# The second gate's sums in the tiles of the bias b2, and half of the last weight chunk in the tiles of the output sums

## The chip, the core and the metric

The kernel runs on one core of a Trainium2 chip. Its engines work side by side, each through its own queue of instructions in order: TensorE (PE, matrix products into the PSUM memory, with PEld for its weight loads), VectorE (DVE), ScalarE (ACT), GpSimd (POOL) and SyncE (SP, which here only issues transfers). The metric is the time of one execution on the device in microseconds (us). A difference of half a per cent, some 5.7 us here, is about what measurements of this kernel can tell from none.

## What is computed

The reference is one layer of an encoder over 256 tokens of width 2048 in float32: windowed attention, then a squared-ReLU MLP with 8192 hidden columns. Each half is scaled and shifted by vectors worked out from a condition `c`, gated by another such vector, added to `alpha * x` and normalised. What the change touches is the second half:

```python
mod = c_act @ mod_w[i] + mod_b[i]
sh_m, sc_m, g_m, sh_f, sc_f, g_f = jnp.split(mod, 6, axis=-1)
...
hff = x * (1.0 + sc_f[:, None, :]) + sh_f[:, None, :]
y = sq_relu_mlp(hff, mlp_w1[i], mlp_b1[i], mlp_w2[i], mlp_b2[i])
x = layer_norm(DEEPNORM_ALPHA * x + (1.0 + g_f[:, None, :]) * y, ln_mlp_g[i], ln_mlp_b[i])
```

The second gate is `g_f`, a product of the condition with a 2048 x 2048 matrix. The bias b2 is `mlp_b2`. The output sums are `y`.

## The kernel before

**Precision.** Every float32 factor is split into a high part (ACT casts it, line 254) and a low part (DVE subtracts the high part from the original, line 225). A product is then two or three fp32r matmuls: `mm3` (lines 497 to 500) is high x high, high x low, low x high.

**The weight stream.** `Stream` (lines 181 to 285) holds one long list of chunks, each 128 x 2048 floats (1 MB), in the order in which they are used. SP loads them into the pool `raws`, which has five buffers at this stage (`loads`, line 203). A chunk of weights is split in two halves of 128 x 1024, whose high and low parts go to the pools `whp` and `wlp` with five buffers each (NHIGH and NLOW, lines 41 and 42). So weights can be up to five halves ahead of TensorE. `pump` (line 230) walks the list; `stop` is a place in it that `pump` does not pass. A chunk planned with `kept` puts its halves into tiles of the pool `g4` and not into the rings, and is split only when it is asked for.

**Modulation chunks.** Chunks of the modulation matrices stand in the same list with a function `use`, which is `Mod.step` (line 322). For the second gate, `m_gf`, all 16 chunks are summed on DVE: two instructions of 128 x 1024 for each chunk (lines 351 to 353), one into each of the two tiles of `part`. Before the first of them, `step` clears the two tiles on POOL (line 334) and loads the gate's bias into row 0 of each through ACT's queue (line 335). `gate` (line 385) later splits the sums, adds up the 128 rows with matmuls and writes the gate into two tiles.

**The MLP** is cut into four blocks of 2048 hidden columns (BLK = 4). The hidden columns of block 0 are worked out first (lines 999 to 1029). Then come, for each block, `ff_hidden` (line 1031, not for block 0) and four calls of `ff_out` (line 1059), one for each chunk c of 512 output columns. One `ff_out` is 96 matmuls of 512 columns: four weight chunks (kg), each with four rows of k, two token tiles t and the three matmuls of `mm3`. Its two sums lie in two PSUM banks out of the pool `psa`, which has five. They are added into the output sums `ys` (lines 1079 to 1083), together with b2 in block 0 (line 1081). The 16 chunks of the gate stand among the weights of block 1, and `gate` is called in block 2 after its second hidden group (line 1048).

**The last chunk** (lines 1112 to 1129) takes c = 3 of block 3 apart: all four weight chunks are asked for, then the whole sum of t = 0 is written, gated, normalised and sent out, then that of t = 1.

**Two pools of tiles of 128 x 1024.** `g4` has 20 buffers. In the last chunk, 8 of them hold the hidden columns (`us`), 4 the residual `xs` and 4 the rows of the last norm (`gb`, line 1092); 4 are left. `g4b` has six buffers and is opened in the memory of early load buffers (line 66). At the MLP it is asked for the four tiles of `ys` (line 1069), two for b2 (line 1070), two for the gate's sums (line 332) and two for the gate itself (line 387).

**Who sets the order.** The order on each engine is not that of the code. A scheduler goes through a model of the run when the program is built: an instruction is put on its engine's queue when its inputs are there in the model and its output tile has a buffer, the earlier in the code first. A tile gets its buffer when its first writer comes up, and gives it back after its last reader. `ORDER_ONLY` edges and `pinned` hold some orders in earlier stages, not here.

Of the kernel before, what the change touches and what calls it, by code (L numbers as in the profile page):

```python
# [12 lines left out]
F32R = mybir.dt.float32r  # L13
# [7 lines left out]
S = 256  # L21
# [9 lines left out]
BLK = 4  # L31
# [16 lines left out]
def hybrid_kernel(ctx: ExitStack, tc: tile.TileContext, a, out: bass.AP):  # L48
# [4 lines left out]
    whp = ctx.enter_context(tc.tile_pool(name="whp", bufs=NHIGH))  # L53
    wlp = ctx.enter_context(tc.tile_pool(name="wlp", bufs=NLOW))
# [11 lines left out]
    def g4b(dt=F32):  # L66
        if not more:
            early.close()
            more.append(ctx.enter_context(tc.tile_pool(name="gen2", bufs=2 * MORE)))
        return more[0].tile([128, 1024], dt, tag="g4b", name="g4b")  # L70

    def g4(dt=F32):
        return gen.tile([128, 1024], dt, tag="g4", name="g4")
# [96 lines left out]

        return add

    def bias_all(src, g4=g4):

        b = [g4(), g4()]
        for h in range(2):
            nc.gpsimd.dma_start(b[h], src[:, h * 1024:h * 1024 + 1024].partition_broadcast(128))
        return lambda c: b[c // 2][:, (c % 2) * 512:(c % 2) * 512 + 512]


    class Stream:
# [15 lines left out]
            self.prev = None  # L197
            self.side = {}

        def plan(self, src, use=None, kept=False):  # L200
            self.q.append((src, use, kept))

        def loads(self):
# [17 lines left out]
        def low(self):  # L221
            n = len(self.ls)
            r, kept = self.src[n]
            l = g4(F32R) if kept else wlp.tile([128, 1024], F32R, name="wl")
            self.pinned(nc.vector.tensor_sub(l, r, f32(self.hs[n])))  # L225
            self.ls.append(l)
            if n % 2:
                self.freed(self.of[n])

        def pump(self, vecs, must=0):  # L230

            while len(self.ls) < must or self.at < len(self.q):
                self.loads()
                n = len(self.hs)
                if len(self.ls) < n - 1 and len(self.ls) - self.used < self.nl or len(self.ls) < min(must, n):
                    self.low()
                    continue
                if self.at >= len(self.q) or self.at == self.stop:
                    return
                assert self.at < len(self.raw)  # L240
                src, use, kept = self.q[self.at]
                if use is not None:
                    if not vecs and n >= must:
                        return
                    vecs = max(vecs - 1, 0)
                    use(self.raw[self.at])
                    self.at += 1
                    self.freed(self.at - 1)
                    continue
                if n >= must and (n - self.used >= self.nh or kept):  # L250
                    return
                h = g4(F32R) if kept else whp.tile([128, 1024], F32R, name="wh")
                s = self.raw[self.at][:, n % 2 * 1024:n % 2 * 1024 + 1024]
                self.pinned(nc.scalar.copy(h, s))  # L254
                self.hs.append(h)
                self.src.append((s, kept))
                self.of.append(self.at)
                self.at += n % 2
# [28 lines left out]
    S = Stream()  # L287
# [4 lines left out]
    class Mod:  # L292
# [29 lines left out]
        def step(self, raw):  # L322
            w, kc, i = self.w, self.kc, self.i
            if i == 0:
                self.ps = psm.tile([128, 512], F32, name="pm")
            r = raw.rearrange("p (k j n) -> p k j n", k=kc // 2 if self.pairs else kc, j=4)
            self.i += 1
            last = self.i == self.n
            per = 1024 // w
            if i == self.start:  # L330

                self.part = [(g4b if self.whole else g4)() for _ in range(2)]
                for n, p in enumerate(self.part):
                    nc.gpsimd.memset(p, 0.0)
                    nc.scalar.dma_start(p[0:1], self.bias[:, n * 1024:n * 1024 + 1024])
            for k in range(kc):
                kt = i * kc + k
                if self.pairs:
                    if k % 2 == 0:
                        cols = [cact[:, kt + j // 2:kt + j // 2 + 1].to_broadcast([128, 32]) for j in range(4)]  # L340
                        self.quad(cols, [r[:, k // 2, j] for j in range(4)], last and k == kc - 2)
                elif i in self.dve:
                    e = min(4 * w, 1024)
                    new = self.part is None
                    if new:
                        self.part = [g4() for _ in range(4 * w // e)]
                    for n, p in enumerate(self.part):
                        s = raw[:, k * 4 * w + n * e:k * 4 * w + n * e + e]
                        if new:
                            nc.vector.tensor_scalar(p[:, :e], s, cact[:, kt:kt + 1], None, op0=OP.mult)  # L350
                        else:
                            nc.vector.scalar_tensor_tensor(p[:, :e], s, cact[:, kt:kt + 1], p[:, :e],  # L352
                                                           op0=OP.mult, op1=OP.add)
                else:
                    stop = last and k == kc - 1 and not self.dve
                    self.quad(cact[:, kt:kt + 1].to_broadcast([128, 32]), [r[:, k, j] for j in range(4)], stop)
            if last and not self.whole:
                if self.dve:
                    self.quad(onesf[:, :32], [self.part[j // per][:, (j % per) * w:(j % per) * w + w]
                                              for j in range(4)], True)  # L360
                self.r = sml.tile([128, 512], F32, name="mrow", bufs=2)
                nc.scalar.copy(self.r[:, :w], self.ps[:, :w])
# [116 lines left out]
    for blk in range(BLK):  # L479
        for f in range(NF):  # L480
            if blk:
                if blk == 1 and f % 2:
                    m_gf.plan()
                S.plan(a["w1b"][(blk - 1) * NF + f])
        for c in range(4):
            for kg in range(4):
                if blk == 1 and kg % 2:
                    m_gf.plan()
                S.plan(a["w2"][blk, c, kg], None, blk == BLK - 1 and c == 3 and kg > 1)


    acc, xts, held, xs = {}, {}, {}, []
# [390 lines left out]
    for n in range(21):  # L883
        j, i = n // 4, n % 4
        if n < 16:
            scores(n)
        for f in todo:
            f()
        todo = []
        if n == 1:  # L890
            S.deep = False
        if n == 5:
            assert all(h is raws for h in S.home[S.at:]), "an early buffer is still in use"
        if n + 2 < len(LATE):
            w = qkv(*LATE[n + 2])
        elif n < 5:
            w = iter((0, 1))
        else:
            if n == 5:
                ys, bo = [g4b() for _ in range(4)], bias_all(a["bo"], g4b)  # L900
            w = project((n - 5) // 4, (n - 5) % 4)
        S.vecs(SLOT_FILL.get(n, 0) if len(LATE) - 2 <= n < 5 else 0)
        mid = mids(n)
        if j < 3:
            if i == 0:
                turn = rope(j + 1, 1)
            if i < 3:
                mid.append(lambda: qA.__setitem__(j + 1, next(turn)))
            if i == 2:
                mid.append(lambda: qhl.__setitem__(j + 1, split_q(qA[j + 1])))  # L910
            if i == 3:
                for h in range(2):
                    mid.append(lambda h=h: qT.__setitem__((j + 1, h), q_heads(qhl[j + 1], h)))
        run(w, mid)
        if 0 < n <= 16 and n % 2 == 0:
            todo.append(values(n - 1))
        if n == 12:
            g1 = gate(m_gm)
        if n == 16:
            warm = sml.tile([128, 1], F32, name="warm")  # L920
            nc.scalar.activation(warm, eps, AF.Sqrt)
            st = [sml.tile([128, 4, 6], F32, name=f"st{t}", bufs=2) for t in range(NT)]
# [144 lines left out]
        return pss  # L1067

    ys = [g4b() for _ in range(4)]
    bf = bias_all(a["b2"], g4b)  # L1070
    for blk in range(BLK - 1):
        if blk:
            us = ff_hidden(blk)
        for c in range(4):
# [9 lines left out]
            if blk == 1:  # L1084
                for t in range(NT):
                    z = part(xs, t, c)
                    nc.vector.scalar_tensor_tensor(z, z, ALPHA, gb[0], op0=OP.mult, op1=OP.mult)
                    nc.vector.scalar_tensor_tensor(z, gb[1], ALPHA, z, op0=OP.mult, op1=OP.add)

    blk = BLK - 1  # L1090
    us = ff_hidden(blk)
# [120 lines left out]
```

## Time and profile before

| what | us |
|---|---|
| median of three runs | 1139.51 (1135.54 to 1139.8) |
| the profiled execution, whole | 1136.72 |
| its span, first to last instruction | 1135.0 |
| TensorE busy | 1088.9 (96% of the span) |
| VectorE busy | 811.0 (71%) |
| ScalarE busy | 546.7 (48%) |
| GpSimd busy | 21.7 (2%) |
| block 0's `ff_out`, c = 0 evicted | 511.8 |
| the first and the last of the 16 loads of the gate's matrix issued | 550.0, 720.7 |
| the last chunk of block 3 begins | 1096.0 |
| TensorE's last matmul begins | 1118.2 |

The profiled execution's 1136.72 us are 1.72 us more than its span. In rows of the timeline, the columns are the start, the duration, the engine, the line of the kernel, the operation, what it writes and reads (the tile's name in the program), how many instructions the row merges, and in brackets how long the engine was idle before and what ended that. A tile of `g4` is shown as `g`, one of `g4b` as `g4b`, a PSUM bank of `psa` as `pa`. A queue's own instruction has a q behind the engine's name. In rows of stages, each engine has its busy time within the stretch and in parentheses its instructions; then come TensorE's granted clock (1.00 is full), the share of the DMA engines' time and GB/s.

### The profile page before, as it was taken

How to read it: one execution, taken by the hardware profiler on the slowest of the kernel's cores; microseconds unless marked ns; L12 is line 12 of the kernel's file. 1: busy time of each engine (PE TensorE's matmuls, PEld its weight loads, DVE VectorE, ACT ScalarE, POOL GpSimd, SP SyncE). 2: the span in 40 equal slices, each digit the busy share in tenths (PEclk: the TensorE clock that was granted, in tenths of full speed). 3: DMA queues.
4: the chain of work that ended last, by engine and by line, in shares of the span. 5: the costliest groups of instructions: out<-in, count | busy, mean ns of one | idle time of the engine just before them, and what ended most of it. 6: DMA issues, size and time to landing. Idle time of an engine off the chain costs nothing.

```text
span 1135.0 us, 15765 instructions
## 1 busy us (share of the span) xinstructions
PE 1088.9 (96%) x6250; PEld 880.2 (78%) x6250; DVE 811.0 (71%) x1121; ACT 546.7 (48%) x852; POOL 21.7 (2%) x40
## 2 busy tenths in 40 slices
PE   8889999799999999999999999999999999999994
PEld 6657667466677699988888887878888888888883
DVE  5587896778899878765577888746666556665656
ACT  5333445676775455553444543335444344444431
POOL 2000000000000000000000010000000000000001
PEclk9999999999999999999999999999999999999997
DMA  9999995656886798655578788854555555557512
GB/s 374 419 420 418 421 392 196 253 186 255 322 305 258 276 366 313 207 187 186 196 290 296 263 303 319 303 206 155 187 187 186 185 190 193 186 187 268 200 38 75
DMA packets 42570, 288.50 MB, mean 254 GB/s; under 512 B 4720, under 2 KB 5360, under 8 KB 8704
## 3 DMA queue, kind: packets, MB, share of 16 engines
q1 hardware_dynamic: 39824, 279.85, 66.8%
q0 software_dynamic: 1792, 6.29, 1.7%
q10 hardware_dynamic: 880, 1.35, 0.3%
q8 instruction: 49, 0.80, 0.3%
q14 instruction: 25, 0.20, 0.0%
HBM read 285.38 MB, written 2.10 MB: 253 GB/s over the span
## 4 chain that ended last, share of the span: by engine, by line
PE 82%; DMA 7%; DVE 6%; ACT 3%; issue 1%; DVEq 0%; ACTq 0%; SPq 0%
PE pa L1042 15%; PE pa L498 14%; PE pa L500 14%; PE pa L499 14%; PE pa L1043 8%; DMA raw<-in_modm 4%; PE pm L314 3%; PE pa L1019 3%; PE pa L1018 3%; PE pa L1020 3%; DVE wl L225 2%; PE pa L789 1%; DMA raw<-in_wqkv 1%; PE pt L774 1%; ACT wh L254 1%
## 5 line engine op out<-in xcount | busy, mean ns | idle before, releaser
L225 DVE TENSOR_TENSOR wl<-raw,wh 128x1024 fp32r<-128x1024 f32 x332 | 404.5, 1224 | 242.0 <-ACT wh L254 241.4
L254 ACT CAST wh<-raw 128x1024 fp32r<-128x1024 f32 x332 | 348.1, 1055 | 457.9 <-PE pa L500 246.9
L498 PE MATMUL pa<-wh,g 128*128 128x512 f32 x816 | 321.5, 395 | 10.9 <-ACT g L534 3.4
L500 PE MATMUL pa<-wh,g 128*128 128x512 f32 x816 | 318.9, 392 | 1.7 <-DVE g L536 1.7
L499 PE MATMUL pa<-wl,g 128*128 128x512 f32 x816 | 319.5, 392 | 0.0
L1042 PE MATMUL pa<-g,wh 128*128 128x512 f32 x768 | 271.8, 399 | 2.9 <-DVE rl L991 2.9
L1043 PE MATMUL pa<-g,wl 128*128 128x256 f32 x768 | 215.7, 281 | 0.0
L498 PEld LDWEIGHTS pa<-wh,g 128*128 128x128 f32 x816 | 153.5, 188 | 52.0 <-issue 6.0
L500 PEld LDWEIGHTS pa<-wh,g 128*128 128x128 f32 x816 | 153.2, 188 | 38.5 <-DVE g L536 3.6
L499 PEld LDWEIGHTS pa<-wl,g 128*128 128x128 f32 x816 | 153.6, 188 | 32.6 <-issue 2.6
L1042 PEld LDWEIGHTS pa<-g,wh 128*128 128x128 f32 x768 | 144.3, 188 | 39.5 <-DVE rl L991 3.6
L1043 PEld LDWEIGHTS pa<-g,wl 128*128 128x128 f32 x768 | 145.1, 189 | 0.2
L1019 PE MATMUL pa<-g,wh 128*128 128x256 f32 x256 | 72.7, 285 | 0.4 <-DVE g L962 0.4
L1018 PE MATMUL pa<-g,wh 128*128 128x256 f32 x256 | 72.5, 286 | 0.0
L1020 PE MATMUL pa<-g,wl 128*128 128x256 f32 x256 | 72.2, 283 | 0.0
L352 DVE SCALAR_TENSOR_TENSOR g<-raw,cact,g 128x1024 f32<-128x1024 f32 x53 | 68.0, 1283 | 0.4
L314 PE MATMUL pm<-raw,cact 128*32 128x256 f32 (+2 forms) x832 | 54.8, 379 | 5.4 <-DMA raw<-in_modm 4.4
L1018 PEld LDWEIGHTS pa<-g,wh 128*128 128x128 f32 x256 | 48.7, 192 | 1.3 <-issue 0.8
L1019 PEld LDWEIGHTS pa<-g,wh 128*128 128x128 f32 x256 | 49.1, 192 | 0.9 <-DVE g L962 0.8
L1020 PEld LDWEIGHTS pa<-g,wl 128*128 128x128 f32 x256 | 49.1, 192 | 0.0
L352 DVE SCALAR_TENSOR_TENSOR g4b<-raw,cact,g4b 128x1024 f32<-128x1024 f32 x32 | 40.6, 1282 | 7.5 <-DMA raw<-in_modgf 5.2
L314 PEld LDWEIGHTS pm<-raw,cact 128*32 128x32 f32 x832 | 21.6, 109 | 27.8 <-issue 12.3
(174 smaller groups left out, 836.7 us busy)
## 6 DMA issues: line engine op xcount, KB each, us to landing
raw<-in_w SPq DMA_DIRECT2D x64, 1024.0 KB, 4.9
raw<-in_w1b SPq DMA_DIRECT2D x48, 1024.0 KB, 4.9
raw<-in_modm SPq DMA_DIRECT2D x32, 1024.0 KB, 14.7
raw<-in_modf SPq DMA_DIRECT2D x32, 1024.0 KB, 7.1
raw<-in_wqkv SPq DMA_DIRECT2D x24, 1024.0 KB, 15.2
raw<-in_modgm SPq DMA_DIRECT2D x16, 1024.0 KB, 6.0
raw<-in_wo SPq DMA_DIRECT2D x16, 1024.0 KB, 5.8
raw<-in_w1a SPq DMA_DIRECT2D x16, 1024.0 KB, 8.1
```

The lines of the kernel that those rows point to most:

```text
L225: self.pinned(nc.vector.tensor_sub(l, r, f32(self.hs[n])))
L254: self.pinned(nc.scalar.copy(h, s))
L314: i = nc.tensor.matmul(self.ps[32 * j:32 * j + 32, :w], lhsT[j] if type(lhsT) is list else lhsT, rhs[j], start=self.first, stop=stop)
L352: nc.vector.scalar_tensor_tensor(p[:, :e], s, cact[:, kt:kt + 1], p[:, :e], op0=OP.mult, op1=OP.add)
L498: nc.tensor.matmul(ps, xh, wh, start=start, stop=False)
L499: nc.tensor.matmul(ps, xh, wl, start=False, stop=False)
L500: S.prev = nc.tensor.matmul(ps, xl, wh, start=False, stop=stop).ins
L1018: nc.tensor.matmul(o, wh(w, 128), hh, start=new, stop=False)
L1019: nc.tensor.matmul(o, wh(w, 128), hl, start=False, stop=False)
L1020: nc.tensor.matmul(o, wl(w, 128), hh, start=False, stop=end)
L1042: nc.tensor.matmul(ps, wh(k, 128), hb, start=k == 0, stop=False)
L1043: nc.tensor.matmul(ps[:, :256], wl(k, 128), hb[:, :256], start=False, stop=k == NK - 1)
```

## The change

- `bias_all` gets its two tiles from its caller instead of taking them from a pool.
- The two tiles of the gate's sums are taken where the output sums are, ahead of block 0, and b2 is loaded into the same two tiles. `step` no longer takes tiles for the second gate; it clears those two when its first chunk comes up, which is after the last read of b2.
- So that the clearing stands behind the reads of b2 in the code, `pump` stops at the gate's first chunk (`first_gf`) until block 0 is through.
- `kept` becomes a number. Of the last weight chunks (block 3, c = 3), kg = 2 goes to `g4` as before (1) and kg = 3 to `g4b` (2).

```diff
-    def bias_all(src, g4=g4):
-
-        b = [g4(), g4()]
+    def bias_all(src, b):
+
         for h in range(2):
             nc.gpsimd.dma_start(b[h], src[:, h * 1024:h * 1024 + 1024].partition_broadcast(128))
...
-            l = g4(F32R) if kept else wlp.tile([128, 1024], F32R, name="wl")
+            l = (g4, g4b)[kept - 1](F32R) if kept else wlp.tile([128, 1024], F32R, name="wl")
...
-                h = g4(F32R) if kept else whp.tile([128, 1024], F32R, name="wh")
+                h = (g4, g4b)[kept - 1](F32R) if kept else whp.tile([128, 1024], F32R, name="wh")
...
             if i == self.start:
 
-                self.part = [(g4b if self.whole else g4)() for _ in range(2)]
+                if not self.whole:
+                    self.part = [g4() for _ in range(2)]
                 for n, p in enumerate(self.part):
                     nc.gpsimd.memset(p, 0.0)
                     nc.scalar.dma_start(p[0:1], self.bias[:, n * 1024:n * 1024 + 1024])
...
                 if blk == 1 and f % 2:
+                    if f == 1:
+                        first_gf = len(S.q)
                     m_gf.plan()
...
-                S.plan(a["w2"][blk, c, kg], None, blk == BLK - 1 and c == 3 and kg > 1)
+                S.plan(a["w2"][blk, c, kg], None, max(kg - 1, 0) if blk == BLK - 1 and c == 3 else 0)
...
-                ys, bo = [g4b() for _ in range(4)], bias_all(a["bo"], g4b)
+                ys, bo = [g4b() for _ in range(4)], bias_all(a["bo"], [g4b(), g4b()])
...
     ys = [g4b() for _ in range(4)]
-    bf = bias_all(a["b2"], g4b)
+    m_gf.part = [g4b(), g4b()]
+    bf = bias_all(a["b2"], m_gf.part)
+    S.stop = first_gf
     for blk in range(BLK - 1):
...
                     nc.vector.scalar_tensor_tensor(z, gb[1], ALPHA, z, op0=OP.mult, op1=OP.add)
+        S.stop = 0
```

More of the change, by code (lines that the diff above doesn't have):

```diff
@@ L198, in __init__, with plan @@
             self.side = {}
-        def plan(self, src, use=None, kept=False):
+        def plan(self, src, use=None, kept=0):
             self.q.append((src, use, kept))
```

## The prediction

> **What bounds the kernel now.** I read the page's head first, then the stages.
>
> ```profile
> span 1135.0 us, 15765 instructions
> PE 1088.9 (96%) x6250; PEld 880.2 (78%) x6250; DVE 811.0 (71%) x1121; ACT 546.7 (48%) x852; POOL 21.7 (2%) x40
> ```
>
> ```profile
> 500.00:1080.00 580.00, 574.77 (x2872) 485.68 (x2872) 383.62 (x455) 255.52 (x311) 7.40 (x13) 1.00 0.64 223
> 680.00:700.00 20.00, 17.64 (x78) 14.27 (x78) 16.66 (x20) 6.35 (x6) 1.34 (x3) 1.00 0.91 323
> 760.00:780.00 20.00, 17.13 (x94) 14.19 (x93) 13.13 (x20) 11.47 (x18) 0.00 (x0) 1.00 0.39 136
> 1120.00:1136.00 16.00, 0.00 (x0) 0.00 (x0) 11.22 (x19) 1.56 (x3) 3.27 (x2) 0.59 0.35 131
> ```
>
> TensorE sets the time. In the MLP (500 to 1080) it is idle for 580.00 - 574.77 = 5.23 us only. The two 20 us stretches hold all of that: 2.36 and 2.87 us. Behind its last matmul comes a tail in which DVE works. So the change can win those 5.23 us and a part of the tail, and nothing else in the MLP. Next, what ends each gap in the timeline of TensorE, and where block 0's sums are evicted (line 1081) in that of DVE, with the gate's reading of its sums (line 392), and the clearings of these sums on POOL:
>
> ```profile
> 693.45 0.50 PE L498 MATMUL pa<-wh,g 128*128 128x512 f32 x1 [2.36 <-DVE g4b L1083]
> 765.92 0.50 PE L1042 MATMUL pa<-g,wh 128*128 128x512 f32 x1 [2.61 <-DVE rl L991]
> 773.73 0.50 PE L1042 MATMUL pa<-g,wh 128*128 128x512 f32 x1 [0.26 <-DVE rl L991]
> ```
>
> ```profile
> 511.77 1.28 DVE L1081 TENSOR_TENSOR g4b<-pa,g4b 128x512 f32<-128x512 f32 x2
> 533.54 1.28 DVE L1081 TENSOR_TENSOR g4b<-pa,g4b 128x512 f32<-128x512 f32 x2
> 555.29 1.28 DVE L1081 TENSOR_TENSOR g4b<-pa,g4b 128x512 f32<-128x512 f32 x2
> 769.13 1.28 DVE L1081 TENSOR_TENSOR g4b<-pa,g4b 128x512 f32<-128x512 f32 x2
> 770.33 1.28 DVE L1083 TENSOR_TENSOR g4b<-g4b,pa 128x512 f32<-128x512 f32 x2
> L392 DVE TENSOR_TENSOR g<-g4b,g x4: 684/686/692, 767.3 to 773.6; 128x512 fp32r<-128x512 f32 x4
> ```
>
> ```profile
> 383.59 0.95 POOL L334 MEMSET g4b<- 128x1024 f32 x1 [40.29 <-issue]
> 534.88 0.96 POOL L334 MEMSET g4b<- 128x1024 f32 x1 [150.33 <-DVE g4b L1081]
> ```
>
> Three evictions come 21.76 us apart, so the fourth was due at 555.29 + 21.76 = 577.1. It comes at 769, 192 us late. The clearings tell why. `g4b` has six buffers: b2 held two, the gate's first sum took one at 383.59, three chunks of `ys` the rest; the buffer that b2 gave back at 534.8 went to the second sum. So the fourth chunk of `ys` had no buffer until the gate had read its sums (from 767.3). Until then block 0's sums for c = 3 stayed in **two of the five banks** of `psa`, and from 757 on block 1's in two more. TensorE therefore waited for a bank: at 691 between c = 0 and c = 1 (two sums end, two begin, three banks), at 763 between two hidden groups with one bank left, and briefly at 773.
>
> **Part 1: sums and b2 share tiles.** Now `g4b` is asked for 2 + 4 tiles, which is six: the fourth eviction finds its buffer and comes at about 577, and all five banks go round. The first and second wait need a shortage of banks, so both should go: 2.36 + 2.61. The third stands where `gate` asks for four banks more; I count it as gone too, 0.26, since the evictions at 769 and 770 (2.4 us of DVE just ahead of it) leave that place. Ends for these gaps: 0 won (each comes back) and 5.23; I take **-5.2**. DVE does the same work.
>
> What is added is a wait. The second tile is read by block 0 until the fourth eviction ends, 577.1 + 1.28 = 578.4. Only then can it be cleared and its bias row loaded:
>
> ```profile
> 555.78 1.06 ACT L254 CAST wh<-raw 128x1024 fp32r<-128x1024 f32 x1 [1.66 <-PE pa L500]
> 555.79 0.56 ACTq L335 DMA_DIRECT2D g4b<-in_modgfb x2
> 558.50 1.06 ACT L254 CAST wh<-raw 128x1024 fp32r<-128x1024 f32 x1 [1.66 <-PE pa L500]
> ```
>
> ```profile
> 556.87 1.23 DVE L225 TENSOR_TENSOR wl<-raw,wh 128x1024 fp32r<-128x1024 f32 x1 [0.30 <-ACT wh L254]
> 560.26 1.29 DVE L352 SCALAR_TENSOR_TENSOR g4b<-raw,cact,g4b 128x1024 f32<-128x1024 f32 x1 [2.16 <-DMA g4b<-in_modgfb]
> 563.73 1.28 DVE L352 SCALAR_TENSOR_TENSOR g4b<-raw,cact,g4b 128x1024 f32<-128x1024 f32 x1
> 555.41 7.63 SPq L209 DMA_DIRECT2D raw<-in_w1b x2
> 565.04 0.33 SPq L209 DMA_DIRECT2D raw<-in_modgf x1
> ```
>
> The time to landing of all loads into `g4b`, and of the gate's chunks:
>
> ```profile
> DMA to landing us min/median/max: 5.3/6.3/7.4
> DMA to landing us min/median/max: 6.4/6.9/7.5
> ```
>
> 578.4 + 0.96 (POOL) = 579.3 for the issue from ACT's queue; the bias was in use 4.5 us after its issue before, and the loads of `g4b` (this row has the large ones too) took up to 7.4: the second sum can start at 584 to 587. Before, it started at 563.73. Three queues feel this. ACT has the issue between its casts. DVE may stand at the waiting sum, as it did for 2.16 us ahead of 560.26; the 580 us stretch shows no TensorE idle time for that. SP's queue feels it most: the load at 565.04 began when the sum at 563.73 gave its buffer back. With the gate's first chunk in its buffer until 586 + 1.3, the next loads of the gate pile up in the five buffers, and the weights pass through three or two. I followed the list through: each weight buffer is given back every 5.44 us (two halves of 558.50 - 555.78 = 2.72); from f = 1 at 555.4 on, f = 2 goes out at 561, the gate's second chunk at 566, f = 3 at 572, f = 4 at 577, the gate's third at 582.5, and f = 5 only with the release near 588, some 11 us late. TensorE needs f = 5 at 577.1 + 5 x 5.44 = 604.3; its first half needs 1.06 (ACT), 1.23 (DVE) and a load of up to 7.5: issue by 594.5. That leaves **6 us**, so I cost the wait at 0. Cover: five halves of weights ahead, 13.6 us. If it were gone, every us of lateness would be one of TensorE. [...]
>
> The stop itself costs nothing that I can find: the casts above are released by TensorE giving back a buffer, not by their place in the code, and the gate's first tile (b2's columns of c = 0 and 1, read by 534.8) can be cleared 44 us ahead of the second.
>
> **Part 2: kg = 3 in the tiles of `ys`.** The tail, by the timelines of ACT, PE and DVE, and line 1101, the last reader of `ys`:
>
> ```profile
> 1105.71 1.06 ACT L254 CAST g<-raw 128x1024 fp32r<-128x1024 f32 x1 [11.18 <-PE pa L500]
> 1110.10 1.06 ACT L254 CAST g<-raw 128x1024 fp32r<-128x1024 f32 x1 [3.33 <-PE pa L500]
> ```
>
> ```profile
> 1095.99 0.39 PE L498 MATMUL pa<-wh,g 128*128 128x512 f32 x1
> 1101.43 0.39 PE L498 MATMUL pa<-g,g 128*128 128x512 f32 x1
> 1104.15 0.39 PE L498 MATMUL pa<-wh,g 128*128 128x512 f32 x1
> 1113.84 0.62 PE L500 MATMUL pa<-g,g 128*128 128x512 f32 x2
> 1118.15 0.39 PE L500 MATMUL pa<-g,g 128*128 128x512 f32 x1
> ```
>
> ```profile
> 1114.27 0.69 DVE L797 TENSOR_TENSOR tmp<-pa,g4b 128x512 f32<-128x512 f32 x1 [1.52 <-PE pa L500]
> 1119.78 0.69 DVE L797 TENSOR_TENSOR tmp<-pa,g4b 128x512 f32<-128x512 f32 x1
> 1120.38 3.08 DVE L1127 SCALAR_TENSOR_TENSOR g<-g,r,g 128x512 f32<-128x512 f32 x3
> 1123.38 0.68 DVE L798 TENSOR_TENSOR g<-g,tmp 128x512 f32<-128x512 f32 x1
> 1128.28 3.08 DVE L1127 SCALAR_TENSOR_TENSOR g<-g,r,g 128x512 f32<-128x512 f32 x3
> ```
>
> ```profile
> L1101 DVE TENSOR_TENSOR g4b<-g4b x8: 685/686/689, 875.9 to 943.5; 128x512 f32<-128x512 f32 x8
> ```
>
> The last two casts wait for TensorE to free tiles of `g4` (four were left, kg = 2 has them). So at 1104.15, behind kg 0, 1 and 2 of t = 0, TensorE goes over to t = 1, and t = 0's sum ends only near 1114, 4.3 us ahead of t = 1's. Both norms then meet on DVE. `ys` was read for the last time by 944.2 (line 1101), so the new tiles are free 150 us early and kg = 3 is split as soon as it has landed. Then t = 0 runs through. One matmul takes (1101.43 - 1095.99) / 24 = 0.2267 us. t = 0's last starts at 1095.99 + 47 x 0.2267 = 1106.6, t = 1's last at + 95 x 0.2267 = 1117.5, not 1118.15. From the last matmul to `tmp` it is 1114.27 - 1113.84 = 0.43 us, then 0.69 for that instruction, and from line 798 to DVE's end 1128.28 + 3.08 - 1123.38 = 7.98, as measured for t = 1. t = 0 is through by 1106.6 + 9.1 = 1115.8, under TensorE's work; t = 1 ends at 1117.5 + 9.1 = 1126.6 where it ended at 1131.36: **-4.7**. What follows (out, 1135.0 - 1131.36 = 3.64) stays. The ends: 0, if TensorE alternates all the same, and -4.7. The four casts and subtractions that come early (1.06 on ACT and 1.23 on DVE a half) fit into the rings' 2.72 us cadence.
>
> **Sum.** -5.2 - 4.7 = -9.9: span 1125.1, the profiled execution 1126.8. The median shown, 1139.51, is 2.8 above the profiled execution's 1136.72 with nothing in the trace to say why, so I put the time half of that up: **1128**.
>
> **Rivals.**
> - *Half of part 1 comes back.* At 691 and 766 DVE is also busy (16.66 and 13.13 of 20), and `gate` asks for four banks at once. With the tail's 4.7 and 0 to 2.6 of the gaps: 1130.5 to 1133. For it: DVE's share. Against: DVE had 3.3 us free in that stretch, and the rows name a bank's eviction. Chance 0.12.
> - *The tail stays*, since the model puts kg = 3 late on DVE or TensorE alternates for another cause: -5.2, 1132.7. Against: the tiles are free long before. 0.07.
> - *No change*, for instance because another tile takes the sixth buffer and c = 3 stays in its banks: 1137 to 1139.5. 0.05.
> - *Slower: weights starve.* If the gate's first chunk holds its buffer past 594.5, TensorE waits from f = 5 on. At 604 the loss is 10 us and the gain is gone, past that the kernel is slower, as it could be if ACT's queue held the bias's issue behind casts that wait for TensorE: 1139 to 1145. [...] 0.06.
>
> **Chances.** The forecast has 0.70, 1125 to 1131. Faster by over 0.5% (5.7 us, about what a measurement can tell): the forecast and half of the first rival, 0.76. Within: 0.18. Slower: 0.06. The range runs from a little under the full gain on the lowest run, 1135.54 - 9.9 = 1125.6 (three runs need not hold the lowest), to the cases with one part alone: 1124 to 1134.
>
> **What would show it.** Right: all eight of line 1081 by 580; a clearing near 579; no wait for lines 1083 and 991 on TensorE; four casts into `g4b` before 1095; the last two `tmp` 10.9 us apart, the first under TensorE's work. Wrong: a wait for line 225 or for `in_w1b` on TensorE between 582 and 610, casts into `g4b` after 1100, or a bank's wait at the gate.

## The result and the profile after

| | median, us | lowest to highest | runs |
|---|---|---|---|
| before | 1138.44 | 1135.54 to 1139.80 | 4 |
| changed | 1125.25 | 1123.28 to 1126.88 | 4 |

The runs of the kernel before are the three of the prediction's median and one more. The ratio is 0.9887, with an interval of 0.986 to 0.9913: faster by 1.1%. The changed kernel's profiled execution took 1126.88 us, with a span of 1125.2 (1135.0 before). The line numbers have moved: `mm3` is now lines 500 to 502, the MLP's evictions are lines 1085 and 1087, `tmp` is line 799, the last norm's final line is 1132 and the weight cast is line 253.

The head of the changed kernel's page, and then its stages; the three stretches that held TensorE's waits come first, in the columns described above:

```profile
span 1125.2 us, 15752 instructions
PE 1088.7 (97%) x6250; PEld 880.2 (78%) x6250; DVE 809.9 (72%) x1121; ACT 545.2 (48%) x852; POOL 21.9 (2%) x40
```

```profile
500.00:1080.00 580.00, 579.90 (x2896) 490.11 (x2895) 387.17 (x459) 258.56 (x315) 8.36 (x14) 1.00 0.64 225
680.00:700.00 20.00, 20.00 (x90) 16.58 (x89) 17.34 (x20) 7.45 (x8) 1.54 (x3) 1.00 0.91 320
760.00:780.00 20.00, 19.90 (x108) 16.37 (x107) 12.89 (x20) 12.98 (x20) 0.00 (x0) 1.00 0.45 158
```

TensorE is now idle for 580.00 - 579.90 = 0.10 us of the MLP, where it was idle for 5.23. Both banks' waits are gone. The busy times of the engines have hardly moved; the span shrank because waits left it.

The timelines of DVE, POOL and ACT at the place of the added wait:

```profile
511.85 1.28 DVE L1085 TENSOR_TENSOR g4b<-pa,g4b 128x512 f32<-128x512 f32 x2
577.12 1.28 DVE L1085 TENSOR_TENSOR g4b<-pa,g4b 128x512 f32<-128x512 f32 x2
582.59 1.28 DVE L352 SCALAR_TENSOR_TENSOR g4b<-raw,cact,g4b 128x1024 f32<-128x1024 f32 x1
```

```profile
534.95 0.96 POOL L334 MEMSET g4b<- 128x1024 f32 x1 [191.59 <-DVE g4b L1085]
578.47 0.96 POOL L334 MEMSET g4b<- 128x1024 f32 x1 [42.56 <-DVE g4b L1085]
```

```profile
579.46 0.23 ACTq L335 DMA_DIRECT2D g4b<-in_modgfb  x1
```

The fourth eviction of block 0 comes at 577.12 instead of 769.13, as the other three had led one to expect. The second tile is cleared at 578.47, its bias is sent for at 579.46, and the second sum runs at 582.59 with no idle time ahead of it. All the added waits together cost TensorE nothing here.

The tail, in the timelines of ACT, DVE and PE:

```profile
1079.60 1.05 ACT L253 CAST g4b<-raw 128x1024 fp32r<-128x1024 f32 x1 [0.90 <-DMA raw<-in_w]
1081.50 1.05 ACT L253 CAST g4b<-raw 128x1024 fp32r<-128x1024 f32 x1
```

```profile
1101.93 0.69 DVE L799 TENSOR_TENSOR tmp<-pa,g4b 128x512 f32<-128x512 f32 x1 [7.69 <-PE pa L502]
1107.57 3.11 DVE L1132 SCALAR_TENSOR_TENSOR g<-g,r,g 128x512 f32<-128x512 f32 x3
1112.81 0.69 DVE L799 TENSOR_TENSOR tmp<-pa,g4b 128x512 f32<-128x512 f32 x1 [2.13 <-PE pa L502]
1118.44 3.08 DVE L1132 SCALAR_TENSOR_TENSOR g<-g,r,g 128x512 f32<-128x512 f32 x3
```

```profile
1112.38 0.39 PE L502 MATMUL pa<-g4b,g 128*128 128x512 f32 x1
```

The halves of kg = 3 are cast by 1082.6, ahead of the last chunk. The two sums end 1112.81 - 1101.93 = 10.9 us apart, so the first norm is over (1107.57 + 3.11 = 1110.7) before the second sum arrives. From the last matmul's start to DVE's end it is 1118.44 + 3.08 - 1112.38 = 9.1 us, where it was 1131.36 - 1118.15 = 13.2.

### The profile page after: what moved, and what is told of

Read it like the earlier page. It is cut to its first block, busy times and chain, and to the rows that moved or that the text cites. A ratio compares the mean times of both kernels' runs of the same rounds, so it can differ in the third digit from the quotient of the medians.

```text
span 1125.2 us, 15752 instructions
## 1 busy us (share of the span) xinstructions
PE 1088.7 (97%) x6250; PEld 880.2 (78%) x6250; DVE 809.9 (72%) x1121; ACT 545.2 (48%) x852; POOL 21.9 (2%) x40
## 4 chain that ended last, share of the span: by engine, by line
PE 85%; DMA 8%; DVE 4%; ACT 2%; issue 0%; DVEq 0%; ACTq 0%; SPq 0%
PE pa L1044 16%; PE pa L500 15%; PE pa L502 15%; PE pa L501 15%; PE pa L1045 8%; DMA raw<-in_modm 4%; PE pm L313 3%; PE pa L1021 3%; PE pa L1020 3%; PE pa L1022 3%; DMA raw<-in_wqkv 2%; PE pa L791 2%; PE pt L776 1%; DVE wl L224 1%; ACT wh L253 1%; PE pa L737 1%
```

## The experiments

In each profile I take two points: block 0's first eviction (511.77 in the kernel before), and the end of the span. Between them lies all that the change was to win. What differs ahead of that point, which comes at 508.6 to 511.9 in all these profiles, is left out by it. The table has every run; the ratios are against runs of the kernel before on the same chip, and 1138.44 is the median of that kernel on the chip of `changed` alone.

| run | median, us | ratio to before | first eviction to end, us | TensorE idle, 500 to 1080, us |
|---|---|---|---|---|
| before | 1138.44 | | 623.2 | 5.23 |
| changed | 1125.25 | 0.9887 (0.986 to 0.9913) | 613.35 | 0.10 |
| changed_again | 1125.73 | 0.9892 (0.9873 to 0.9911) | 611.9 | 0.10 |
| p1_sums_only | 1130.04 | 0.9928 (0.9911 to 0.9945) | 618.1 | 0.11 |
| p2_tail_only | 1132.88 | 0.9950 (0.993 to 0.9969) | 621.2 | 6.20 |
| gb_in_ys_tiles | 1125.66 | 0.9891 (0.9876 to 0.9907) | 613.35 | 0.11 |
| hold_two_banks | 1126.42 | 0.9892 (0.9851 to 0.9933) | 615.45 | 2.97 |
| hold_four_banks | 1129.68 | 0.9927 (0.9898 to 0.9955) | 618.2 | 4.89 |
| clear_late_10 | 1125.92 | 0.9888 (0.9846 to 0.9929) | 613.4 | 0.11 |
| clear_late_20 | 1124.92 | 0.9879 (0.9839 to 0.9919) | 611.9 | 0.10 |
| clear_late_60 | 1150.04 (one run; before 1138.71, one run) | | 637.0 | 21.44 |

### Each part alone, and the second part another way

`p1_sums_only` is the changed kernel with both of the last weight chunks in `g4`, as before:

```diff
-                S.plan(a["w2"][blk, c, kg], None, max(kg - 1, 0) if blk == BLK - 1 and c == 3 else 0)
+                S.plan(a["w2"][blk, c, kg], None, int(blk == BLK - 1 and c == 3 and kg > 1))
```

> Part 1 alone: the gate's sums share b2's tiles, both kept weight chunks go to g4 as in the kernel before. If the late eviction of block 0's c = 3 and the two PSUM banks that it holds are the cause of the three waits, TensorE's idle time in 500 to 1080 falls from 5.23 us to under 0.4, all eight evictions of block 0 are done by 580, and the tail stays as before (the last two tmp 5.5 us apart, the last two casts released by TensorE): span 1135.0 - 5.2 = 1129.8. If the two parts lean on each other (the gaps go only with the tail's tiles), the idle time stays above 2 us and the span at 1132 or more.

`p2_tail_only` is the kernel before with only the numbered `kept`:

```diff
-            l = g4(F32R) if kept else wlp.tile([128, 1024], F32R, name="wl")
+            l = (g4, g4b)[kept - 1](F32R) if kept else wlp.tile([128, 1024], F32R, name="wl")
...
-                S.plan(a["w2"][blk, c, kg], None, blk == BLK - 1 and c == 3 and kg > 1)
+                S.plan(a["w2"][blk, c, kg], None, max(kg - 1, 0) if blk == BLK - 1 and c == 3 else 0)
```

> Part 2 alone: kg = 3 of the last chunk goes to g4b, sums and b2 have their own tiles as before. If the tail was long because the last two halves had no tile, the last two tmp are 10.9 us apart and DVE ends 9.1 us behind the start of the last matmul: -4.6, span 1130.4, with the waits of 2.36, 2.61 and 0.26 us unchanged. If the tail's gain needs part 1, the casts of kg = 3 still wait for TensorE and the span stays within 1 us of 1135.

`gb_in_ys_tiles` leaves both weight chunks in `g4`, and makes room there by putting the rows of the last norm into `g4b`:

```diff
-                S.plan(a["w2"][blk, c, kg], None, max(kg - 1, 0) if blk == BLK - 1 and c == 3 else 0)
+                S.plan(a["w2"][blk, c, kg], None, int(blk == BLK - 1 and c == 3 and kg > 1))
...
-    gb = [[g4(), g4()], [g4(), g4()]]
+    gb = [[g4b(), g4b()], [g4b(), g4b()]]
```

> As the changed kernel, but the other way round: the four rows of the last norm (gb) lie in the tiles that the output sums leave, and kg = 2 and kg = 3 both in g4, where eight tiles are then free. If the number of free tiles is all that counts, the tail is that of the changed kernel: last two tmp 10.9 us apart, span 1125.2 within 0.7. If it matters which tiles, or gb's loads come late, the tail is longer: 1127 or more.

`changed_again` is the changed kernel, timed beside these three:

> The changed kernel once more, on the chip of the other three. Its trace has given 9.8 us less span than the one before; the medians differ by 13.2. If the 3.4 us between are scatter of single executions, the medians here differ by some 10 (ratio 0.991); if the profiled executions hide a part of the gain, by 13 again (0.9885).

The MLP and the tail of `p1_sums_only`, in its stages and in its DVE timeline:

```profile
500.00:1080.00 580.00, 579.89 (x2895) 490.11 (x2894) 387.15 (x459) 258.60 (x315) 8.34 (x14) 1.00 0.64 225
```

```profile
1108.72 0.69 DVE L799 TENSOR_TENSOR tmp<-pa,g4b 128x512 f32<-128x512 f32 x1 [1.52 <-PE pa L502]
1114.24 0.69 DVE L799 TENSOR_TENSOR tmp<-pa,g4b 128x512 f32<-128x512 f32 x1
```

Its MLP is that of the changed kernel (0.11 us idle), and its tail that of the kernel before: the two `tmp` are 5.5 us apart. From the first eviction on it ends 623.2 - 618.1 = 5.1 us ahead of the kernel before and 618.1 - 613.35 = 4.7 behind the changed one. So in these profiles the parts add up, and each has the size of its term. `gb_in_ys_tiles` ends where the changed kernel does (613.35 for both). What counts for the tail is that all four of its weight halves have tiles; which pool they come from does not.

By the medians the first part is worth more: 0.72% of 1138.0 is 8.2 us, with an interval of 6.3 to 10.1, and the second 5.7 (3.5 to 8.0). The interval of the first does not hold 5.2. `changed_again` says the same of the whole: its median is 12.3 us under that of the kernel before, nearer to 13 than to the 10 that scatter alone would have given. The PE timeline of `p2_tail_only` points to why, with its stages and the two `tmp` of its tail beside it:

```profile
692.08 0.50 PE L498 MATMUL pa<-wh,g 128*128 128x512 f32 x1 [3.33 <-DVE g4b L1083]
```

```profile
690.00:700.00 10.00, 7.92 (x28) 6.35 (x29) 9.38 (x11) 2.10 (x2) 0.52 (x1) 0.83 0.87 301
```

```profile
1107.34 0.69 DVE L797 TENSOR_TENSOR tmp<-pa,g4b 128x512 f32<-128x512 f32 x1 [7.69 <-PE pa L500]
1118.22 0.69 DVE L797 TENSOR_TENSOR tmp<-pa,g4b 128x512 f32<-128x512 f32 x1 [2.13 <-PE pa L500]
```

Nothing was changed at 691, yet the wait is 3.33 us and not the 2.36 that was expected, and the granted clock behind it falls to 0.83 over 10 us. This is 0.17 x 10 = 1.7 us of TensorE's work, on top of the wait. So this profile ends only 623.2 - 621.2 = 2.0 us ahead of the kernel before. With the longer wait (6.20 - 5.23 = 1.0) and the 1.7 added back, its part is worth 4.7, as in the other comparison, and its two `tmp` are 10.9 us apart. That its span came out at 1130.6, where 1130.4 was expected, is luck: its first eviction came 2.3 us earlier (509.43), which made up for most of the 2.7.

### Are the banks the cause of the waits?

The rival: TensorE waits because DVE is late with its evictions at 691 and 766, for reasons of its own. Here block 0's fourth eviction stays early, but its two banks are not given back until DVE has read one column of each in `gate` (at 771.0). The second kernel also holds block 1's two (there all four are read from 766.5 to 768.1). The results of these reads are not used.

```diff
+    hold = []
     def gate(m):
...
             nc.vector.tensor_sub(p[:, 512:], v, f32(p[:, :512]))
+        for ps in hold:
+            nc.vector.tensor_add(sml.tile([128, 1], F32, name="late"), ps[:, :1], f32(hl[-1][:, 1023:1024]))
...
-            for t, ps in enumerate(ff_out(blk, us, c)):
+            pss = ff_out(blk, us, c)
+            hold.extend(pss if c == 3 and blk in (0,) else [])
+            for t, ps in enumerate(pss):
```

(`hold_four_banks` has `blk in (0, 1)`.)

> The changed kernel with the two PSUM banks of block 0's c = 3 held until the second gate has split its sums, by two tiny late readers (128x1); the sums themselves are evicted on time, so DVE has no late work of weight. If banks are the cause, a wait of about 2.4 us comes back at the first handover of block 1 (c = 0 to c = 1, near 691) and little at the gate, since block 1's own last sums are evicted: idle in 500 to 1080 of 2.4 to 3.5 us, span near 1128. If DVE's late evictions were the cause, no wait comes back: under 0.4.

> The same, and the two banks of block 1's c = 3 are held as well until the gate has split its sums: one bank is left for the hidden groups of block 2, as in the kernel before, but without its four late evictions on DVE. If banks are the cause, the wait of 2.6 us near 760 comes back too: idle of about 5 us in 500 to 1080, span near 1130. If DVE's burst made it, idle stays at the value of the run with two banks.

The PE timeline of `hold_two_banks`, and then that of `hold_four_banks`:

```profile
691.32 0.50 PE L504 MATMUL pa<-wh,g 128*128 128x512 f32 x1 [2.35 <-DVE g4b L1093]
```

```profile
690.02 0.50 PE L504 MATMUL pa<-wh,g 128*128 128x512 f32 x1 [2.14 <-DVE g4b L1093]
762.52 0.50 PE L1048 MATMUL pa<-g,wh 128*128 128x512 f32 x1 [2.61 <-DVE rl L997]
```

Two banks held bring back the first wait, in the place and nearly the size of before (2.35 and 2.36); the rest of the 2.97 lies at the gate, 0.44 of it in one wait that ends at 768.75. Four bring back both; the second is 2.61 in `hold_four_banks` and in the kernel before. All else that the change did is still in these kernels. The waits are therefore the shortage of banks, and DVE's eviction in the row is the one that TensorE needs because only three, or one, are left. The time goes with them: 4.9 us over four banks. The medians show that loss too: 1129.68 against 1125.92 and 1124.92 of `clear_late_10` and `clear_late_20`, which ran on the same chip and have no such wait. For two banks they show little (1126.42), though its trace lost 2.1; its interval, 0.9851 to 0.9933, holds either. Both spans are some 3 us under those expected (1125.1 for 1128, 1126.8 for 1130), since the first eviction came 2.2 and 3.3 us earlier than in the profile of the changed kernel.

### How much room does the added wait have?

The second gate tile is cleared 11 times over instead of once (`clear_late_20`: 21 times), which delays the bias row and with it the first use of the gate's first chunk:

```diff
-                    nc.gpsimd.memset(p, 0.0)
+                    for _ in range(11 if n and self.whole else 1):
+                        nc.gpsimd.memset(p, 0.0)
```

The expectation of the first speaks of both tiles; only the second was delayed, as only that one lies on the path.

> The changed kernel with each of the two gate tiles cleared eleven times over on POOL instead of once: the second sum can start 10 x 0.96 = 9.6 us later. The gate's first chunk is then given back near 593.5 instead of 583.9. If weights starve only past 594.5, as worked out in the prediction, TensorE loses at most 1 us: span 1125 to 1126.5. If DVE standing at the waiting sum is what counts, subtractions come late and several us are lost: 1128 or more.

> The same with 21 clearings: the second sum 19.2 us later, the gate's first chunk given back near 603. By the prediction's account of the five load buffers TensorE then waits for the weights of group f = 5 for 603 - 594.5 = 8.5 us (6 us if the load takes the 5 us it usually takes): a wait for lines 224 or 253 or for the load itself between 600 and 612, span 1131 to 1134. If there is more cover than the account has, for instance because the queue of loads is not held up, the loss is under 2 us: 1127 or less.

Neither lost anything: 0.11 and 0.10 us of TensorE idle. The timelines of POOL, DVE and SP's queue in `clear_late_20`:

```profile
578.21 21.22 POOL L335 MEMSET g4b<- 128x1024 f32 x21 [42.56 <-DVE g4b L1086]
```

```profile
602.12 1.28 DVE L353 SCALAR_TENSOR_TENSOR g4b<-raw,cact,g4b 128x1024 f32<-128x1024 f32 x1
```

```profile
582.39 0.33 SPq L208 DMA_DIRECT2D raw<-in_modgf  x1
588.04 6.04 SPq L208 DMA_DIRECT2D raw<-in_w1b  x2
599.35 0.33 SPq L208 DMA_DIRECT2D raw<-in_modgf  x1
603.43 1.85 SPq L208 DMA_DIRECT2D raw<-in_w1b  x2
```

The chunk's buffer is held to 602.12 + 1.28 = 603.4, nearly 20 us longer than in the changed kernel. Yet two weight loads, f = 5 and f = 6, go out in between (the first at 588.04): each takes the buffer that an earlier weight chunk gave back. In the changed kernel f = 5 did go out with the gate's chunk given back (at 583.89), but here it went out only 4 us later without that. So f = 5 does not hang on the gate's chunk, as the prediction had it. By this reading it is f = 9 that does, and the price of a late release begins some 25 us further out. A still later clearing, 61 times over (to 639.6), tests that account against the prediction's:

> The changed kernel with the second gate tile cleared 61 times over, so that the second sum starts some 61 us later and the gate's first chunk keeps its load buffer until about 644. With 21 clearings no time was lost: the loads of the weights went out with each other's releases. New account: each chunk of the gate that is loaded meanwhile keeps one of the five buffers; the loads go out in the order f = 5, 6, gate, 7, 8, gate, 9, so the fifth buffer is gone with the gate's chunk ahead of f = 9, and f = 9 waits for the release at 644. TensorE needs it at 577.1 + 9 x 5.68 = 628; 644 + 5 for the load + 2.3 for the split = 651: about 23 us lost, in one wait near 628 to 651, span near 1148. The prediction's account (f = 5 starves) would put the wait at 604 and the loss at 49 us, span near 1174. If the buffers never run out: span 1125.

The profile of `clear_late_60`, in the timelines of SP's queue, of DVE and of PE:

```profile
587.77 6.04 SPq L208 DMA_DIRECT2D raw<-in_w1b  x2
...
604.74 8.69 SPq L208 DMA_DIRECT2D raw<-in_w1b  x2
621.91 0.33 SPq L208 DMA_DIRECT2D raw<-in_modgf  x1
642.57 1.65 SPq L208 DMA_DIRECT2D raw<-in_w1b  x2
```

```profile
641.25 6.57 DVE L353 SCALAR_TENSOR_TENSOR g4b<-raw,cact,g4b 128x1024 f32<-128x1024 f32 x5 [10.96 <-DMA g4b<-in_modgfb]
```

```profile
648.79 0.80 PE L1045 MATMUL pa<-g,wh 128*128 128x512 f32 x1 [20.87 <-ACT wh L253]
```

Four weight loads (f = 5 to 8) went out while the chunk was held. The fifth is issued at 642.57, just as the first sum of five, at 641.25, is through with it. TensorE stands for 20.87 us from 627.9 on and goes on 648.79 - 642.57 = 6.2 us after the issue. By this, f = 9 would have had to go out by 627.9 - 6.2 = 621.7 to cost no wait. In the changed kernel the chunk is given back at 582.59 + 1.28 = 583.9: that makes **some 38 us of room**, where the prediction's 594.5 would have left 10.6. Releases at 603.4 and at 642.5 were measured, none between. That the loss begins at 621.7 and grows by one us for each us of delay is worked out from one run, in which SP's queue issued no load between 621.91 and 642.57, and not shown.

From the first eviction on, this kernel takes 637.0 - 613.35 = 23.65 us more than the changed one, and 23 were expected, but not in these terms. The wait was to last until 651 and ended at 648.8; the rest is mainly the clock, which by the matmuls' lengths stood at about one half for 6.3 us behind it (the last section) and was not in that account.

### Three more executions of the kernel before

If the wait at 691 is not the same in each execution, one profile of the kernel before says too little. So the unchanged kernel before was profiled three times more.

> The kernel before, unchanged, looked at again. Its medians lie 12 to 13 us above those of the changed kernel, where the two traces differ by 9.8. Theory: the wait for a bank near 691 is not always 2.36 us; in the run of part 2 alone it was 3.33 us, and the granted clock behind it fell to 0.83 for ten microseconds. Then looks differ in this wait, and those with over 3 us show a clock below 1.00 in the 20 us behind it and take some 2.5 us more from the first eviction of block 0 to the end (625.7 instead of 623.2). Rival: the difference lies ahead of the MLP: the first eviction of block 0 comes later than 512.5 us, and the rest takes 623.2 as in the first look.

> As the look before it: the wait near 691 over 3 us goes with a clock below 1.00 and 625 us or more from the first eviction of block 0 to the end; the rival has 623.2 there in every look.

> As the two looks before it: the wait near 691 over 3 us goes with a clock below 1.00 and 625 us or more from the first eviction of block 0 to the end; the rival has 623.2 there in every look.

The PE timelines of `before_look_1`, `_2` and `_3`, and of the first also the stretch in which its clock was low:

```profile
692.84 0.50 PE L498 MATMUL pa<-wh,g 128*128 128x512 f32 x1 [2.58 <-DVE g4b L1083]
765.31 0.50 PE L1042 MATMUL pa<-g,wh 128*128 128x512 f32 x1 [2.61 <-DVE rl L991]
```

```profile
766.80:770.20 3.40, 3.40 (x13) 2.92 (x12) 3.40 (x6) 2.21 (x4) 0.00 (x0) 0.51 0.00 0
```

```profile
692.88 0.50 PE L498 MATMUL pa<-wh,g 128*128 128x512 f32 x1 [2.27 <-DVE g4b L1083]
```

```profile
694.42 0.50 PE L498 MATMUL pa<-wh,g 128*128 128x512 f32 x1 [3.58 <-DVE g4b L1083]
```

| profile | wait at 691, us | at 766, us | clock low behind | first eviction to end, us | whole execution, us |
|---|---|---|---|---|---|
| before | 2.36 | 2.61 | neither | 623.2 | 1136.72 |
| before_look_1 | 2.58 | 2.61 | 766 | 623.55 | 1136.18 |
| before_look_2 | 2.27 | 2.61 | neither | 621.7 | 1134.71 |
| before_look_3 | 3.58 | 2.61 | 691 | 626.2 | 1139.40 |
| p2_tail_only | 3.33 | 2.61 | 691 | 621.2 | 1132.28 |

The wait at 691 varies from 2.27 to 3.58 us, that at 766 not at all. The rival of the expectation, 623.2 in each of them, falls. The theory holds for `before_look_3`; the fall of the clock behind 766 in `before_look_1` was not forecast. What makes the wait vary stands just ahead of it on DVE, in the timeline of `before_look_3`:

```profile
686.07 1.28 DVE L352 SCALAR_TENSOR_TENSOR g4b<-raw,cact,g4b 128x1024 f32<-128x1024 f32 x1 [3.68 <-DMA raw<-in_modgf]
...
693.68 1.28 DVE L1083 TENSOR_TENSOR g4b<-g4b,pa 128x512 f32<-128x512 f32 x2
```

DVE stands for 3.68 us until a chunk of the gate's matrix has landed, and the eviction that TensorE needs is queued behind that. The eviction comes as late as the transfer: in each of the five profiles TensorE goes on 8.34 or 8.35 us after this sum's start (694.42 - 686.07 here, 693.45 - 685.11 in the first profile). With five banks going round, nobody waits for it: in the changed kernel DVE stood for 2.55 us at the same place, and in `p1_sums_only` for 3.55, with TensorE at full work in both.

## Why the prediction was right, and where it was not

**What bounds the kernel: right.** Only the 5.23 us in the MLP and the tail could be won, and both were.

**Part 1, the cause: right.** All eight evictions of block 0 come by 580, the second clearing at 578.47, and both banks' waits are gone. The runs with banks held show that the banks, not DVE's load at that place, were the cause. The rival *half of part 1 comes back* falls with this. The third wait, counted as gone on a weaker argument, is gone too; the 0.10 that is left is another, among the gate's own matmuls (line 397, at 768).

**Part 1, the size: too small.** "-5.2" is right for the execution that was profiled (5.1 with `p1_sums_only`). But it took that execution's waits as those of every run. Three of the five profiles that have the waits had the clock fall behind one of them, and each such fall cost 1.7 us (0.17 x 10 in `p2_tail_only` and `before_look_3`, 0.49 x 3.4 in `before_look_1`). Over the five, the wait at 691 is 2.82 us on average, that at 766 with the small one behind it 2.87, and the falls add 3 x 1.7 / 5 = 1.0. That makes 6.7 us for a usual run, less 0.1 that is left: 6.6, inside the 6.3 to 10.1 of the medians. With the tail's 4.7 it is 11.3, and inside the intervals of the whole change too (1138.44 x 0.0087 = 9.9 at the least). The medians themselves have 12.3 and 13.2, so 1 to 2 us stay without a measured cause; five profiles are few for an average.

**The added wait: right at 0, for a wrong reason.** The step that failed is "f = 5 only with the release near 588", and with it "6 us left" and the rival's price "at 604 the loss is 10 us". With a release at 603.4 the loss was 0. I had let the gate's waiting chunks take each buffer that came free; the queue showed f = 5 to f = 8 going out past the one held. The mechanism of the rival does exist, and `clear_late_60` is slower than the kernel before by it (one run each), but it had not set in with a release at 603.4, where 594.5 was the prediction's limit; by the one run that shows it, it decides from about 621.7 on. The bias too was in use sooner than I took it: at most 3.1 us after its issue (579.46 to 582.59), for the 4.5 that I took from the kernel before, so the second sum ran ahead of my 584 to 587. In `clear_late_60`, where SP's queue issued no load between 621.91 and 642.57, it was in use 641.25 - 639.61 = 1.6 us after its issue.

**Part 2: right, term by term.** t = 0 runs through, the first norm is under TensorE's work, and 9.1 us from the last matmul to DVE's end was the measured figure. *The tail stays* falls.

**The sum.** The trace came out at 1125.2 where 1125.1 stood in the prediction, and the profiled execution at 1126.88 for 1126.8. That it is so close is in part luck: `changed_again`, the same kernel, has a span of 1122.3, and the profile that the prediction started from had no fall of the clock. The median came out at 1125.25 for 1128. Half of the 2.8 us between the median shown and the profiled execution was added there as a thing that would stay. By the profiles taken since, part of it was the waits themselves, which were longer in some of them or had a slower clock behind them. That part went with them.

**What stays open.** The time from the first eviction to the end has one more source of scatter, and both kernels have it: the pace of block 2's hidden groups. The stages of the changed kernel, and of `changed_again`, which is the same kernel:

```profile
800.00:820.00 20.00, 20.00 (x115) 17.34 (x114) 12.58 (x18) 9.79 (x15) 0.00 (x0) 1.00 0.50 176
```

```profile
800.00:820.00 20.00, 20.00 (x117) 17.52 (x116) 12.73 (x19) 9.75 (x14) 0.00 (x0) 1.00 0.55 186
```

TensorE is never idle in either and its clock is full, but it gets through 115 or 117 matmuls in 20 us. Executions with the first pace end after 613.35 to 613.4 us (changed, `gb_in_ys_tiles`, `clear_late_10`), with the second after 611.9 (`changed_again`, `clear_late_20`). Every profile has the same 6250 matmuls, so the difference is not one of missing records. Of the kernel before, `before_look_1` and `_2` had the faster pace. With 1.5 us for it, 1.7 for a fall of the clock and the wait as measured, the three come to 623.2 + 0.22 + 1.7 - 1.5 = 623.6, 623.2 - 0.09 - 1.5 = 621.6 and 623.2 + 1.22 + 1.7 = 626.1, each within 0.1 us of its profile. `hold_two_banks` does not fit as well: by the same sum it should be at 613.35 + 2.97 - 0.10 - 1.5 = 614.7 and is at 615.45. What sets the pace was not found.

A seventh buffer for `g4b` in the kernel before would have been another way to undo the shortage. It was not tried; the three early load buffers whose memory the pool takes hold just six such tiles.

## What to carry to other kernels

When a matmul waits for an eviction, ask not only why the eviction is late but who holds the other banks: here a missing buffer of another pool had kept two of five since 577, over 110 us ahead of the first wait. Tiles whose lives follow each other (a bias, then a gate's sums) can share a buffer at the price of one wait, and that wait is safe as far as the load queue runs on past it, which a delayed clearing can test (here a release at 603.4 cost nothing, one at 642.5 a wait of 20.87 us). A wait that hangs on a transfer was not a constant here (2.27 to 3.58 us): take two or three profiles before its size goes into a sum.

## What the runs showed of the hardware

- Behind some of TensorE's waits in the MLP the granted clock fell, behind most it did not. Of the waits of the kernel before and its relatives, those of 3.33 and 3.58 us were each followed by a slow stretch; of the 2.61 us waits at 766, one in six was (`before_look_1`), and none of the five of 2.14 to 2.58 at 691. What decides between them was not shown: in the other five profiles the same 2.61 us had none behind it. In `before_look_1` the slow stretch starts 1.5 us after TensorE resumes at 765.31, as the matmuls' lengths show in the PE timeline, and lasts 3.4 us at a granted clock of 0.51:

```profile
766.47 0.40 PE L1042 MATMUL pa<-g,wh 128*128 128x512 f32 x1
...
767.42 0.63 PE L1042 MATMUL pa<-g,wh 128*128 128x512 f32 x1
...
769.34 0.63 PE L1042 MATMUL pa<-g,wh 128*128 128x512 f32 x1
...
770.47 0.40 PE L1042 MATMUL pa<-g,wh 128*128 128x512 f32 x1
```

- After the wait of 20.87 us in `clear_late_60` the matmuls of 512 columns are 0.63 us long until 654.9, as in the stretch at 0.51, and 0.40 from 655.35 on: by this the clock stayed at about one half for 6.3 us, longer than the 3.4 us of `before_look_1`.
- Clearing one tile 61 times kept GpSimd busy for 61.65 us and did not slow the sum on DVE that ran beside it: the one of 128 x 1024 took 1.28 us at 604.96 under that work, as it did at 582.59 in the changed kernel.
